# A running sum in one PSUM bank for the seven-product form, and a second group in four gate-and-up pairs of a decoder trunk

## The chip, the cores and the metric

The kernel runs on one core of a Trainium2 chip. The metric is the time of one execution on the device in microseconds (us), as the median of several runs. The profiled execution is a run of its own, with its own time. The engines are called as in the profile: PE (matrix products), PEld (loading of PE's stationary operand), DVE (vector), ACT (scalar), POOL (GpSimd) and SP (which here issues loads).

## The reference

The reference is a trunk of two decoder layers over 256 positions with 2048 channels, batch 1, all in float32. Of each layer only the products matter here:

```
h = rmsnorm(x);  proj = h @ w_in               # conv pair, q, k, v, two branch gates
m = sigmoid(g_A) * y_A + sigmoid(g_B) * y_B;   x += m @ w_out
gate, up = split(rmsnorm(x) @ w_gate_up)       # 2048 -> 2 x 5632
x += (silu(gate) * up) @ w_down                # 5632 -> 2048
x += sigmoid(rmsnorm(x) @ w_ple_gate) * (p[i] @ w_ple_proj)
```

y_A comes from a convolution branch, y_B from attention with eight heads. A last rmsnorm follows the second layer.

## The kernel before, in words

**Chunks and splits.** A weight matrix is cut into chunks of 512 output columns. The positions are two blocks of 128. The sum over the input rows is cut into groups of 512 rows (four tiles of 128). A half of a group, 256 rows by 512 columns, is one load of 512 KB into a raw tile (`fetch`, L133, issued by SP); there are eight raw tiles. Every float32 operand is split into a high part and a low part: `split` (L138) lets ACT copy raw to the high part wh (L141) and DVE subtract it to get the low part wl (L142). There are five wh and five wl tiles. A product of two split operands is three matmuls (L184, L185, L186): high times high, high times low and low times high. Activations are split in the same way and lie in pair tiles. A plain group of two chunks is four loads, four splits and 48 matmuls of 512 columns.

**The seven-product form.** `fast_chunks` (L238) takes two chunks w1 and w2 at once, and for some of the groups (the list `fast`) it uses seven products in place of eight. For one such group the blocks of the activations are B11, B12, B21, B22 (row halves of the group by position blocks) and those of the weights a11, a12 (from w1) and a21, a22 (from w2). The activation side has four sums, made once by `Fast.make` (L362): M1 = B11 - B12, T2 = M1 + B22, T3 = B22 - B12 and N4X = B21 - T2. On the weight side the tile sm starts as a21 and receives a11 by an accumulating load that POOL issues (L276). The seven products are, in the code's order:

- p1 = B11 with a11
- c21, N4X with a22
- c11, B21 with a12
- q7, T3 with sm, which is a21 + a11
- q6, T2 with sm after `add(sm, sm, a22)` (DVE, L287, recorded at the helper's line 271)
- q5, M1 with a11 after `sub(a11, sm, a11)` (L289, recorded at line 272)
- c12, B22 with a12 after `add(a12, a12, sm)` (L291, recorded at line 271)

Each is one split and six matmuls, 42 matmuls in all. c11, c12 and c21 are added in PSUM to the plain groups' sums. p1, q5, q6 and q7 have a bank of their own each (tiles ms; there are four). After the last group ACT copies p1 out (L293), and DVE makes from it p1 - q6, p1 - q6 + q7 and both of these plus q5 (L294 to L297), which are added to the plain sums or subtracted from them (L300, L304).

**The order of the work.** `go` is one plain step: it loads a half, splits it and multiplies it with both position blocks (12 matmuls). One or two such steps stand between the products of a group. After the groups come the rest of w1's plain steps, then the first result is used (`first`, L301), then w2's plain steps. Instructions are planned ahead of the run: each engine has a fixed order, close to that of the code, but an instruction whose operands are late by the planner's costs is overtaken by one that is ready. Tiles are handed out in that plan too, so a load waits in SP's queue until its raw tile is free.

**Where it is used.** There are 48 calls in the two layers: gates of the two branches, `w_out`, gate and up, down, and the last gate of a layer. The feed-forward part is done in three parts of 3, 4 and 4 chunks of 512 hidden columns (`FFN_PARTS`); in each part the gate-and-up pairs of its chunks come first, then the down projection. A gate-and-up pair uses two groups (L922), but the first pair of the second and third part uses one, and the first of the first part is plain. In all 80 groups run in the seven-product form.

Of the kernel before, what the change touches and what calls it, by code (L numbers as in the profile page):

```python
# [12 lines left out]
AF = mybir.ActivationFunctionType  # L13
ALU = mybir.AluOpType
# [31 lines left out]
def trunk(ctx, tc, xT, xR, pT, wI, wF, wC, wA, wOut, wGU, wD, wPG, wPP, vec, bF, gF, out):  # L46
    nc = tc.nc
# [11 lines left out]
    act, dve, pe = nc.scalar, nc.vector, nc.tensor  # L59
    uid = iter(range(1 << 30))  # L60

    def pair(dtype=F32):
        return pairs.tile([P, 2, 512], dtype, tag="pair", name=f"pair{next(uid)}")
# [69 lines left out]
    def fetch(src):  # L133
        raw = raws.tile([P, 2, 512], F32, tag="raw", name=f"raw{next(uid)}")
        nc.sync.dma_start(raw.rearrange("p k n -> p (k n)"), src)
        return raw
# [34 lines left out]


    class Sum:
        def __init__(self, n, bank):
            self.n, self.left, self.bank = n, n, bank

        @property
        def t(self):
# [2 lines left out]
        def add(self, xh, xl, wh, wl):  # L181
            start = self.left == self.n
            self.left -= 1
            pe.matmul(self.t, lhsT=xh, rhs=wh, start=start, stop=False)  # L184
            pe.matmul(self.t, lhsT=xh, rhs=wl, start=False, stop=False)  # L185
            pe.matmul(self.t, lhsT=xl, rhs=wh, start=False, stop=self.left == 0)  # L186

    def once(make):

        made = []  # L190

        def get():
            if not made:
                made.append(make())
            return made[0]

        return get

    def sums_of_blocks(n1, n2=None):
        t = once(bank_mm)  # L200
        return t, Sum(n1, lambda: t()[:, 0, :]), Sum(n1 if n2 is None else n2, lambda: t()[:, 1, :])
# [36 lines left out]
    def fast_chunks(fast, w1, w2, xs, ks, first, by_block=None):  # L238

        nf, nk = 2 * len(fast), 4 * len(ks)
        p1, q5, q6, q7 = (Sum(nf, once(bank_ms)) for _ in range(4))
        c1, c11, c12 = sums_of_blocks(nf + nk)
        c2, c21, c22 = sums_of_blocks(nf + nk, nk)
        if by_block is not None:
            c22 = Sum(nk, once(bank_ms))
        left = deque()
        for w, sums in ((w1, (c11, c12)), (w2, (c21, c22))):
            for g, k0 in enumerate(ks):  # L250
                for half in range(2):
                    left.append((w[len(fast) + g][:, half * 1024 : (half + 1) * 1024], sums, k0 + 2 * half))
        state = dict(quiet=True)

        def go(n=1):
            for _ in range(n):
                src, sums, k0 = left.popleft()
                parts = split(fetch(src))
                await_x(xs, (k0, k0 + 1))
                plain(sums, xs, k0, parts)  # L260
                if not state["quiet"]:
                    fill(CONV // 2 + len(left) % 2)
                    run()

        def product(to, operand, raw):
            h, l = split(raw)
            xh, xl = operand
            for kk in range(2):
                to.add(xh(kk), xl(kk), h[:, kk, :], l[:, kk, :])

        add = lambda o, a, b: dve.tensor_tensor(o, a, b, op=ALU.add)  # L271
        sub = lambda o, a, b: dve.tensor_tensor(o, a, b, op=ALU.subtract)  # L272
        u1, u2 = pair(), pair()
        for g, f in enumerate(fast):
            a11, sm = fetch(w1[g][:, :1024]), fetch(w2[g][:, :1024])
            nc.gpsimd.dma_start(sm.rearrange("p k n -> p (k n)"), w1[g][:, :1024], accum_op=ALU.add)  # L276
            a22, a12 = fetch(w2[g][:, 1024:]), fetch(w1[g][:, 1024:])
            product(p1, f(B11), a11)
            product(c21, f(N4X), a22)
            go()  # L280
            product(c11, f(B21), a12)
            if len(left) > 2 * len(ks):
                go()
            if nk == 8 and len(fast) == 1:
                run()
            product(q7, f(T3), sm)
            add(sm, sm, a22)  # L287
            product(q6, f(T2), sm)
            sub(a11, sm, a11)  # L289
            product(q5, f(M1), a11)  # L290
            add(a12, a12, sm)  # L291
            product(c12, f(B22), a12)
        act.activation(u1[:, 0, :], p1.t, AF.Copy)  # L293
        sub(u1[:, 1, :], u1[:, 0, :], q6.t)  # L294
        add(u2[:, 0, :], u1[:, 1, :], q7.t)
        add(u1[:, 1, :], u1[:, 1, :], q5.t)
        add(u2[:, 1, :], u2[:, 0, :], q5.t)  # L297
        state["quiet"] = False
        go(len(left) - 2 * len(ks))
        add(u1, u1, c1())  # L300
        first(u1)  # L301
        if by_block is None:
            go(len(left))
            sub(u2, c2(), u2)  # L304
            return u2
        go(len(left) - 4)
        held = [(split(fetch(src)), k0) for src, _, k0 in left]
        for b, c in enumerate((c21, c22)):
            for parts, k0 in held:
                plain([c, c], xs, k0, parts, [b])  # L310
            sub(u2[:, b, :], c.t, u2[:, b, :])
            by_block(b, u2)
# [25 lines left out]

        return (lambda b: o[:, b * P : (b + 1) * P]), (lambda b: o[:, S + b * P : S + (b + 1) * P])

    B11, B12, B21, B22, M1, T2, T3, N4X = range(8)

    class Fast:

# [17 lines left out]
        def make(self):  # L362
            f = lambda n: self.f[n // 4][:, n % 4]
            sub = lambda o, a, b, op: dve.tensor_tensor(f(o), f(a), f(b), op=op)  # L364
            sub(M1, B11, B12, ALU.subtract)
            sub(T2, M1, B22, ALU.add)
            sub(T3, B22, B12, ALU.subtract)
            sub(N4X, B21, T2, ALU.subtract)
            self.h, self.l = [], []
            for t in self.f:  # L370
                h, l = (pair(F32R).rearrange("p a b -> p (a b)") for _ in range(2))
                t = t.rearrange("p n k s -> p (n k s)")
                act.activation(h, t, AF.Copy)  # L373
                dve.tensor_tensor(l, t, h.bitcast(F32), op=ALU.subtract)  # L374
                self.h.append(h.rearrange("p (n k s) -> p n k s", n=4, k=2))
                self.l.append(l.rearrange("p (n k s) -> p n k s", n=4, k=2))
            self.f = None
# [167 lines left out]
    for i in range(L):  # L545
# [356 lines left out]
        c0 = 0  # L902
        for part, nch in enumerate(FFN_PARTS):
            hid = {}
            fast_hid = [Fast() for _ in range(nch - 2)]
            for c in range(c0, c0 + nch):
                w1, w2 = wGU[i, 2 * c], wGU[i, 2 * c + 1]
                o = pair() if c == 0 else None

                def gate(g):  # L910
                    nonlocal o
                    if o is None:
                        o = g
                    for b in range(2):
                        act.activation(o[:, b, :], g[:, b, :], AF.Silu, scale=norm.r(b))

                if c == 0:
                    gate(chunk(by_four(w1), norm.xs))
                    up = chunk(by_four(w2), norm.xs)
                else:  # L920
                    nf = 1 if c == c0 else 2
                    up = fast_chunks(norm.fast[:nf], w1, w2, norm.xs, range(4 * nf, KD, 4), gate)  # L922
                for b in range(2):
                    dve.scalar_tensor_tensor(
                        o[:, b, :], up[:, b, :], norm.r(b), o[:, b, :], op0=ALU.mult, op1=ALU.mult
                    )
                turns.append(
                    lambda c=c, o=o, hid=hid, fast=fast_hid[c - c0] if c - c0 < len(fast_hid) else None:
                    operand(hid, 4 * c, lambda b: o[:, b, :], fast)
                )  # L930
            for n in range(0, N4, 2):
                await_x(hid, (4 * c0,))
                on = after if part == len(FFN_PARTS) - 1 else None
                nf = 1 if n == 0 else len(fast_hid)
                onto_x(on, n + 1)(
                    fast_chunks(
                        fast_hid[:nf], wD[i, n][c0 : c0 + nch], wD[i, n + 1][c0 : c0 + nch], hid,
                        range(4 * (c0 + nf), 4 * (c0 + nch), 4), onto_x(on, n),
                    )
                )  # L940
            c0 += nch
            if part == len(FFN_PARTS) - 2:
                pin = tmp().rearrange("p (k s) -> p k s", k=2)
                nc.sync.dma_start(pin, pT[i])
                po = pair(F32R)
                halves(po, pin)
                ps = {k: by_blocks(po[:, k, :]) for k in range(2)}
# [119 lines left out]
```

## Time and profile before

| what | value |
|---|---|
| median of 3 runs | 2793.24 us (2793.18 to 2793.36) |
| profiled execution, its own time | 2793.7 us |
| its span, first to last instruction | 2791.8 us |
| PE, DVE, ACT busy | 2773.9, 2507.1, 1660.0 us |
| matmuls of 512 columns in L184 to L186 | 11712 |
| splits by ACT and DVE (L141, L142) | 1254 |
| DMA | 585.24 MB, mean 210 GB/s |

A row of a group reads: line, engine, operation, tile written <- tiles read, shape and count; then the busy time in us, the mean of one in ns, and the idle time of that engine just before these instructions, with what ended it. A row of waits reads: who waited <- for whom: us in total, times, longest. A row of the timeline has the start and the duration in us. A row of a stage has, after its bounds and its length, the busy time of each engine in it.

### The profile page before, as it was taken

What the parts mean: (1) busy time and instruction counts of PE and PEld (TensorE: products, weight loads), DVE (VectorE), ACT (ScalarE), POOL (GpSimd) and SP (SyncE); (2) the same over time, 40 slices, a digit from 0 to 9 for tenths busy, and PEclk for the clock granted to TensorE, in tenths of its full rate; (3) what the DMA queues carried; (4) which work ended last, traced back from release to release, by engine and by line L of the source; (5) the groups of instructions that cost most, each with busy time, mean ns of one, the idle gap of its engine ahead of it and who ended that gap; (6) DMA issues with size and microseconds to landing.
All of it is one profiled execution on the core that took longest, in us unless ns stands there. A gap on an engine that the chain in (4) does not pass through costs nothing.

```text
span 2791.8 us, 34941 instructions
## 1 busy us (share of the span) xinstructions
PE 2773.9 (99%) x12568; PEld 2293.5 (82%) x12568; DVE 2507.1 (90%) x3003; ACT 1660.0 (59%) x2002; POOL 79.4 (3%) x121
## 2 busy tenths in 40 slices
PE   9999999999999999999999999999999999999998
PEld 7888888888888888888888888888888888888886
DVE  7999889888989988999979988988799899889998
ACT  7445766565556655656754466655665565556565
POOL 0000000000000000000000000000000000000000
PEclk9999999999999999999999999999999999999999
DMA  7555557666676766776655555575666677677674
GB/s 299 188 182 185 199 186 227 198 217 201 217 226 220 227 218 220 224 221 203 215 186 190 185 181 199 189 233 184 228 205 215 216 232 231 203 229 218 217 239 131
DMA packets 161597, 585.24 MB, mean 210 GB/s; under 512 B 18192, under 2 KB 18448, under 8 KB 161168
## 3 DMA queue, kind: packets, MB, share of 16 engines
q1 hardware_dynamic: 149040, 539.50, 56.5%
q0 software_dynamic: 11520, 41.95, 8.3%
q8 instruction: 98, 1.61, 0.2%
q10 hardware_dynamic: 864, 1.57, 0.2%
q14 instruction: 75, 0.61, 0.1%
HBM read 580.85 MB, written 2.10 MB: 209 GB/s over the span
## 4 chain that ended last, share of the span: by engine, by line
PE 93%; DVE 3%; issue 3%; ACT 1%; POOL 0%; POOLq 0%; ACTq 0%; DVEq 0%
PE mm L186 25%; PE mm L185 25%; PE mm L184 25%; PE ms L184 5%; PE ms L185 5%; PE ms L186 5%; PE ms L334 2%; DVE wl L142 1%; DVE raw L271 0%; PE ms L726 0%; ACT wh L141 0%; PE ms L755 0%; DVE pair L374 0%; PE ms L745 0%; DVE pair L271 0%
## 5 line engine op out<-in xcount | busy, mean ns | idle before, releaser
L141 ACT ACTIVATE wh<-raw 128x1024 fp32r<-128x1024 f32 x1254 | 1300.5, 1058 | 1022.7 <-PE mm L186 576.7
L142 DVE TENSOR_TENSOR wl<-raw,wh 128x1024 fp32r<-128x1024 f32 x1254 | 1501.0, 1219 | 212.4 <-ACT wh L141 204.9
L184 PE MATMUL mm<-wh,pair 128*128 128x512 f32 x3224 | 1261.9, 392 | 1.1 <-ACT pair L324 0.7
L185 PE MATMUL mm<-wl,pair 128*128 128x512 f32 x3224 | 1256.6, 390 | 0.9 <-DVE wl L142 0.8
L186 PE MATMUL mm<-wh,pair 128*128 128x512 f32 x3224 | 1256.8, 390 | 0.5 <-DVE pair L325 0.5
L186 PEld LDWEIGHTS mm<-wh,pair 128*128 128x128 f32 x3224 | 605.2, 188 | 128.4 <-DVE pair L325 1.4
L185 PEld LDWEIGHTS mm<-wl,pair 128*128 128x128 f32 x3224 | 605.6, 188 | 126.3 <-DVE wl L142 3.2
L184 PEld LDWEIGHTS mm<-wh,pair 128*128 128x128 f32 x3224 | 605.4, 188 | 126.0 <-ACT pair L324 1.7
L184 PE MATMUL ms<-wh,pair 128*128 128x512 f32 x680 | 265.7, 391 | 0.1
L186 PE MATMUL ms<-wh,pair 128*128 128x512 f32 x680 | 264.7, 389 | 0.0
L185 PE MATMUL ms<-wl,pair 128*128 128x512 f32 x680 | 264.6, 389 | 0.0
L569 DVE SCALAR_TENSOR_TENSOR pair<-pair,vecs,pair 128x256 f32<-128x256 f32 x480 | 201.1, 474 | 0.0
L271 DVE TENSOR_TENSOR raw<-raw,raw 128x1024 f32<-128x1024 f32 x160 | 195.4, 1222 | 2.6
L184 PEld LDWEIGHTS ms<-wh,pair 128*128 128x128 f32 x680 | 127.7, 188 | 28.0 <-ACT pair L998 0.9
L186 PEld LDWEIGHTS ms<-wh,pair 128*128 128x128 f32 x680 | 127.6, 188 | 26.7
L185 PEld LDWEIGHTS ms<-wl,pair 128*128 128x128 f32 x680 | 127.7, 188 | 26.0
L272 DVE TENSOR_TENSOR raw<-raw,raw 128x1024 f32<-128x1024 f32 x80 | 98.0, 1225 | 2.6
L271 DVE TENSOR_TENSOR pair<-pair,ms 128x512 f32<-128x512 f32 x144 | 93.9, 680 | 0.0
L272 DVE TENSOR_TENSOR pair<-mm,pair 128x1024 f32<-128x1024 f32 (+1 forms) x48 | 58.1, 1210 | 11.5 <-PE mm L186 11.4
L271 DVE TENSOR_TENSOR pair<-pair,mm 128x1024 f32<-128x1024 f32 x48 | 58.3, 1215 | 5.5 <-PE mm L186 5.5
L374 DVE TENSOR_TENSOR pair<-pair,pair 128x1024 fp32r<-128x1024 f32 x52 | 62.8, 1217 | 0.0
L373 ACT ACTIVATE pair<-pair 128x1024 fp32r<-128x1024 f32 x52 | 54.3, 1055 | 2.7 <-DVE pair L364 1.6
(168 smaller groups left out, 1065.0 us busy)
## 6 DMA issues: line engine op xcount, KB each, us to landing
raw<-in_wGU_dram SPq DMA_DIRECT2D x352, 512.0 KB, 4.8
raw<-in_wI_dram SPq DMA_DIRECT2D x287, 512.0 KB, 4.0
raw<-in_wD_dram SPq DMA_DIRECT2D x176, 512.0 KB, 4.8
raw<-in_wOut_dram SPq DMA_DIRECT2D x64, 512.0 KB, 4.6
raw<-in_wPG_dram SPq DMA_DIRECT2D x64, 512.0 KB, 4.9
raw<-in_wGU_dram POOLq DMA_DIRECT2D x36, 512.0 KB, 7.9
raw<-in_wA_dram SPq DMA_DIRECT2D x32, 512.0 KB, 4.7
raw<-in_wC_dram SPq DMA_DIRECT2D x32, 512.0 KB, 4.9
```

The lines of the kernel that those rows point to most:

```text
L141: act.activation(h, raw, AF.Copy)
L142: dve.tensor_tensor(l, raw, h.bitcast(F32), op=ALU.subtract)
L184: pe.matmul(self.t, lhsT=xh, rhs=wh, start=start, stop=False)
L185: pe.matmul(self.t, lhsT=xh, rhs=wl, start=False, stop=False)
L186: pe.matmul(self.t, lhsT=xl, rhs=wh, start=False, stop=self.left == 0)
L271: add = lambda o, a, b: dve.tensor_tensor(o, a, b, op=ALU.add)
L272: sub = lambda o, a, b: dve.tensor_tensor(o, a, b, op=ALU.subtract)
L334: pe.transpose(pt[:, kk * S + b * P : kk * S + (b + 1) * P], src(b)[:, c : c + P], ident)
L373: act.activation(h, t, AF.Copy)
L374: dve.tensor_tensor(l, t, h.bitcast(F32), op=ALU.subtract)
L569: dve.scalar_tensor_tensor(cv[c], u[c][:, j : j + S], w, cv[c], op0=ALU.mult, op1=ALU.add,)
```

## The change

Two things are changed.

1. The results p1, q6 and q7 get one bank, `chain`, in which they become a running sum. p1 of all groups is multiplied first; ACT copies the bank (p1). Then, group by group, the products with NT2, which is -T2, are added to it; ACT copies it again (p1 - q6). At the end the products with T3 are added, and ACT copies it a third time (p1 - q6 + q7). DVE only adds q5 to two of these. For that `Sum` gets a third argument, the number of places at which the sum may be read, and `Fast.make` makes NT2 in place of T2. The tile sm stays a21 + a11 up to the end, where T3 is multiplied with it; the weight sum for NT2 is written over a22. The accumulating load of the second group is issued within the first group's turn. The tiles u1 and u2 are taken later.
2. The first gate-and-up pair of the second and third part uses two groups, as the others do (`nf = 2`). Over two layers that is four pairs.

```diff
     class Sum:
-        def __init__(self, n, bank):
-            self.n, self.left, self.bank = n, n, bank
+        def __init__(self, n, bank, rests=1):
+
+            self.n, self.left, self.bank, self.rest = n, n, bank, n // rests
...
-            pe.matmul(self.t, lhsT=xl, rhs=wh, start=False, stop=self.left == 0)
+            kw = dict(skip_group_check=self.rest < self.n)
...
+            pe.matmul(self.t, lhsT=xl, rhs=wh, start=False, stop=self.left % self.rest == 0, **kw)
...
-        p1, q5, q6, q7 = (Sum(nf, once(bank_ms)) for _ in range(4))
+        chain, q5 = Sum(3 * nf, once(bank_ms), 3), Sum(nf, once(bank_ms))
...
-        u1, u2 = pair(), pair()
+        def third(g):
+            sm = fetch(w2[g][:, :1024])
+            nc.gpsimd.dma_start(sm.rearrange("p k n -> p (k n)"), w1[g][:, :1024], accum_op=ALU.add)
+            return sm
+
+        s3 = [third(0)]
+        a11s = []
         for g, f in enumerate(fast):
-            a11, sm = fetch(w1[g][:, :1024]), fetch(w2[g][:, :1024])
-            nc.gpsimd.dma_start(sm.rearrange("p k n -> p (k n)"), w1[g][:, :1024], accum_op=ALU.add)
+            a11s.append(fetch(w1[g][:, :1024]))
+            product(chain, f(B11), a11s[g])
+        u1 = pair()
+        act.activation(u1[:, 0, :], chain.t, AF.Copy)
+        for g, f in enumerate(fast):
+            a11, sm = a11s[g], s3[g]
             a22, a12 = fetch(w2[g][:, 1024:]), fetch(w1[g][:, 1024:])
-            product(p1, f(B11), a11)
             product(c21, f(N4X), a22)
             go()
             product(c11, f(B21), a12)
...
-            product(q7, f(T3), sm)
-            add(sm, sm, a22)
-            product(q6, f(T2), sm)
-            sub(a11, sm, a11)
+            if g < len(fast) - 1:
+                s3.append(third(g + 1))
+            add(a22, sm, a22)
+            product(chain, f(NT2), a22)
+            if g == len(fast) - 1:
+                act.activation(u1[:, 1, :], chain.t, AF.Copy)
+            sub(a11, a22, a11)
             product(q5, f(M1), a11)
-            add(a12, a12, sm)
+            add(a12, a12, a22)
             product(c12, f(B22), a12)
-        act.activation(u1[:, 0, :], p1.t, AF.Copy)
-        sub(u1[:, 1, :], u1[:, 0, :], q6.t)
-        add(u2[:, 0, :], u1[:, 1, :], q7.t)
+        for sm, f in zip(s3, fast):
+            product(chain, f(T3), sm)
         add(u1[:, 1, :], u1[:, 1, :], q5.t)
+        u2 = pair()
+        act.activation(u2[:, 0, :], chain.t, AF.Copy)
         add(u2[:, 1, :], u2[:, 0, :], q5.t)
...
-            sub(T2, M1, B22, ALU.add)
             sub(T3, B22, B12, ALU.subtract)
-            sub(N4X, B21, T2, ALU.subtract)
+            dve.scalar_tensor_tensor(f(NT2), f(M1), -1.0, f(B22), op0=ALU.mult, op1=ALU.subtract)
+            sub(N4X, B21, NT2, ALU.add)
...
-                    nf = 1 if c == c0 else 2
+                    nf = 2
```

More of the change, by code (lines that the diff above doesn't have):

```diff
@@ L183, in add @@
             self.left -= 1
-            pe.matmul(self.t, lhsT=xh, rhs=wh, start=start, stop=False)
-            pe.matmul(self.t, lhsT=xh, rhs=wl, start=False, stop=False)
-            pe.matmul(self.t, lhsT=xl, rhs=wh, start=False, stop=self.left == 0)
+            kw = dict(skip_group_check=self.rest < self.n)
+            pe.matmul(self.t, lhsT=xh, rhs=wh, start=start, stop=False, **kw)
+            pe.matmul(self.t, lhsT=xh, rhs=wl, start=False, stop=False, **kw)
+            pe.matmul(self.t, lhsT=xl, rhs=wh, start=False, stop=self.left % self.rest == 0, **kw)
     def once(make):
@@ L339, in by_blocks @@
         return (lambda b: o[:, b * P : (b + 1) * P]), (lambda b: o[:, S + b * P : S + (b + 1) * P])
-    B11, B12, B21, B22, M1, T2, T3, N4X = range(8)
+    B11, B12, B21, B22, M1, NT2, T3, N4X = range(8)
     class Fast:
```

## Prediction

> **What bounds the kernel now.** I read the page's first two parts, then its costliest groups, then the waits, then busy times by stage.
>
> ```profile
> span 2791.8 us, 34941 instructions
> PE 2773.9 (99%) x12568; PEld 2293.5 (82%) x12568; DVE 2507.1 (90%) x3003; ACT 1660.0 (59%) x2002; POOL 79.4 (3%) x121
> PEclk9999999999999999999999999999999999999999
> L142 DVE TENSOR_TENSOR wl<-raw,wh 128x1024 fp32r<-128x1024 f32 x1254 | 1501.0, 1219 | 212.4 <-ACT wh L141 204.9
> L141 ACT ACTIVATE wh<-raw 128x1024 fp32r<-128x1024 f32 x1254 | 1300.5, 1058 | 1022.7 <-PE mm L186 576.7
> ```
>
> PE is busy in every slice at full clock. DVE is second with 90%, an average that hides what matters below. A busy PE isn't proof that it is at its pace, so I take the pace from the timeline. These two rows, from a stretch of back-to-back products, stand 8 rounds of three matmuls (L184, L185, L186) apart:
>
> ```profile
> 774.07 0.39 PE L184 MATMUL mm<-wh,pair 128*128 128x512 f32 x1
> 779.51 0.39 PE L184 MATMUL mm<-wh,pair 128*128 128x512 f32 x1
> ```
>
> 24 matmuls take 779.51 - 774.07 = 5.44 us, so 0.2267 us each. The 0.39 us is the length of one, overlapped with the next. All 11712 such matmuls (3 x 3224 into mm banks, 3 x 680 into ms banks) take 2655 us of the 2791.8 at this pace; most of the rest is transposes, attention and the two ends. What PE waits for in between is little:
>
> ```profile
> ACT wh L141 <- PE mm L186: 576.7, 421, 2.7
> ACT wh L141 <- DVE raw L271: 316.1, 142, 4.9
> PEld mm L185 <- DVE wl L142: 3.2, 7, 0.9
> PEld ms L334 <- DVE xt L881: 2.2, 6, 0.8
> ACT wh L141 <- DMA raw<-in_wGU_dram: 2.2, 1, 2.2
> ```
>
> The producers wait for PE, hardly ever PE for them, and a split waited for a gate-and-up load once. So PE's matmul count is the time, as long as DVE keeps up. The busy times of one first gate-and-up pair (layer 0, part 2) and the two pairs behind it, cut at PE's own borders:
>
> ```profile
> core 0: us, PE busy (x) PEld busy (x) DVE busy (x) ACT busy (x) POOL busy (x), PEclk, DMA share, GB/s
> 790.40:832.56 42.16, 42.16 (x188) 34.92 (x187) 31.93 (x29) 21.45 (x22) 1.70 (x2) 1.00 0.72 224
> 832.56:874.28 41.72, 41.72 (x190) 34.62 (x188) 41.24 (x42) 27.41 (x29) 1.70 (x2) 1.00 0.64 204
> 874.28:916.00 41.72, 41.72 (x189) 34.61 (x188) 41.43 (x42) 27.13 (x29) 1.25 (x2) 1.00 0.72 226
> ```
>
> The first pair, with one group, uses 31.93 of 42.16 us of DVE. The pairs with two groups use 41.24 and 41.43 of 41.72: there DVE has no room at all.
>
> **The second group in four pairs.** A group of 512 rows costs 8 products of 6 matmuls the plain way and 7 in the seven-product form. Two layers with two parts each give 4 pairs, so 4 x 6 = 24 matmuls go, which is just the 5.44 us of the rows above; one pair falls from 186 to 180 matmuls, 42.16 to 40.8 us. [...]
>
> What the group adds: 7 splits in place of 4 and three adds on raw tiles.
>
> ```profile
> L271 DVE TENSOR_TENSOR raw<-raw,raw 128x1024 f32<-128x1024 f32 x160 | 195.4, 1222 | 2.6
> L271 DVE TENSOR_TENSOR pair<-pair,ms 128x512 f32<-128x512 f32 x144 | 93.9, 680 | 0.0
> L272 DVE TENSOR_TENSOR pair<-pair,ms 128x512 f32<-128x512 f32 x48 | 32.6, 680 | 0.0
> L293 ACT ACTIVATE pair<-ms 128x512 f32<-128x512 f32 x48 | 27.7, 578 | 0.0
> L364 DVE TENSOR_TENSOR pair<-pair,pair 128x256 f32<-128x256 f32 x52 | 21.7, 418 | 1.9 <-ACT pair L358 1.8
> L569 DVE SCALAR_TENSOR_TENSOR pair<-pair,vecs,pair 128x256 f32<-128x256 f32 x480 | 201.1, 474 | 0.0
> ```
>
> On DVE that is 3 x 1.22 for splits and 3 x 1.22 for adds, 7.3 us a pair; on ACT 3 x 1.06 = 3.2 us; one more accumulating load of 512 KB on POOL's queue, which is 3% busy. DVE in the first pair then needs 31.93 + 7.3 = 39.2 of 40.8 us before the other part of the change helps. The cover is the 10.2 us in which DVE is idle there now. If it were not usable, because it lies in the plain stretch that is halved, the pair would run at DVE's pace and give back up to its 1.36 us.
>
> **The running sum, in all 48 calls.** Of the four DVE instructions that combine p1, q5, q6 and q7, the subtract of q6 and the add of q7 go: 2 x 0.68 = 1.36 us of DVE a call, 65 us in all. Two more ACT copies of 0.578 come: 1.16 us a call, 55 us in all, on an engine that is 59% busy. PE's products are the same. Beside the first pair's 7.3 us the saving leaves DVE 37.9 of 40.8 us; for the steady pairs 41.24 - 1.36 = 39.9 of 41.72. So DVE stays behind PE as the bound. NT2 by a scalar-tensor-tensor costs at most 474 - 418 = 56 ns more in each of the operands made, under 2 us of DVE in the program and hidden. What the freed time is worth on PE: at most the 3.2 us for splits, whose seven waits lie partly at the start and in attention; I take 0.3 us, one such wait:
>
> ```profile
> 737.51 1.24 DVE wl L142
> 738.79 0.50 PE mm L185
> ```
>
> It is in the chain of waits, and this L185 starts when DVE ends; the pace would have been 0.23.
>
> **Waits that the sum adds.** The bank must be read between its products. The first copy has c21, a plain step, c11 and a second step behind p1 before NT2 writes (36 matmuls, 8.2 us, in a call with two groups). The second copy has only q5 and c12 before T3: 12 matmuls, 2.72 us. Queued on ACT around it are splits; one or two ahead of it make 0.58 + 1.06 or 0.58 + 2.12 = 2.70 us. So its cost is 0 up to two splits ahead, and about 1.06 us a call with three. I take 0, since ACT must itself wait for PE before a sixth split (five tiles of each kind).
>
> **What moves on the queues.** In a two-group call SP's order becomes sm, a11, the second a11, then a22, a12, two plain loads, and sm of the second group. This moves the second a11 ahead of four loads; all hold raw tiles, of which there are eight. sm now stays until T3 at the end, and a22 takes the place of sm as the tile that is added to. Loads already wait for tiles:
>
> ```profile
> SPq L135 <- DVE wl L142: 1666.7, 786, 9.4
> raw<-in_wGU_dram SPq DMA_DIRECT2D x352, 512.0 KB, 4.8
> raw<-in_wGU_dram POOLq DMA_DIRECT2D x36, 512.0 KB, 7.9
> ```
>
> The tightest load is the second group's first plain one. Today it starts when the first add frees a22; afterwards a22 is free only after the third:
>
> ```profile
> 879.89 1.23 DVE L271 TENSOR_TENSOR raw<-raw,raw 128x1024 f32<-128x1024 f32 x1
> 881.14 0.33 SPq L135 DMA_DIRECT2D raw<-in_wGU_dram  x1
> 883.45 1.22 DVE L271 TENSOR_TENSOR raw<-raw,raw 128x1024 f32<-128x1024 f32 x1
> 891.96 0.19 PEld L185 LDWEIGHTS mm<-wl,pair 128*128 128x128 f32 x1
> ```
>
> The split of T3 and its product, and p1 of the second group, leave this stretch. The third add then ends about 1.2 us sooner than 884.67, at 883.5, and PE wants the tile 2 x 1.36 us sooner than 891.96, at 889.24. With 4.8 us to land and 1.06 + 1.22 for the split it is ready at 890.6: 1.4 us late. If c11, whose load isn't late, is put ahead of it (1.36 us of PE), it is on time within 0.05 us. The price is thus 0 to 1.4 us in each of 36 two-group calls (32 now and 4 new). I take 0, nearest to the row of today, in which no split waits for such a load, because the order is planned before the run and a planner that sees the tile come late puts the ready product first. The second sm is still the eighth tile and has c21, two plain steps and c11 more before its use, over 8 us.
>
> Sum: -5.44 - 0.3 = -5.7 us. The profiled execution took 2793.7 us (span 2791.8 and 1.9 around it), so 2788.0; the median of the runs is 0.46 us below the profiled one, so **2787.5 us**.
>
> **Rivals.**
> 1. Late loads, slower. Mechanism and place as above: eight raw tiles, the plain load after the third add. Break-even is 5.7 / 36 = 0.16 us a call; at 0.4 us, that is at 5.2 us to land without the better order, 14.4 - 5.7 = +8.7 us, 2802. For it: the 1666.7 us that loads wait for tiles. Against it: one wait for a gate-and-up load in the whole trace.
> 2. The bank, slower. T3 waits for the second copy, with three splits ahead of it: 48 x 1.06 = 51 us, 2838. Against it: in the row of L293 today's copies had 0.0 us of idle time before them. [...]
> 3. The cover is gone: the first pairs run at DVE's pace and all 5.44 us are given back, 2793. For it: two-group pairs fill DVE to 99% today. Against it: 2.9 us of room after both parts.
> 4. More than the matmuls: the freed DVE time also ends most waits for splits and residuals, 2 us, 2785.8.
>
> That the change doesn't do what it says can't be for the count: 24 matmuls fewer is fixed by the code.
>
> **How the numbers follow.** A measurement of this kernel can tell about 0.2%, 5.59 us, from no change: the border is 2787.65, almost on my forecast. Forecast (gain between 4.4 and 6.7): 0.55, of which 0.35 falls over the border. Rival 4: 0.08. A gain partly or wholly eaten (rival 3, or small waits): 0.19. Rivals 1 and 2 beyond 0.2%: 0.12 and 0.06. Faster 0.35 + 0.08 = 0.43; same 0.20 + 0.19 = 0.39; slower 0.18. The range goes from rival 4's 2785.8 to 2796.0, where late loads cost 0.23 us in 36 calls; beyond it lie most of the slower cases. The forecast's own range is 2786.5 to 2788.8.
>
> **What would show it.** Right: 11688 large matmuls at 0.227 us; the four first pairs at 40.8 us; DVE near 2507 - 65 + 29 = 2471 us and ACT near 1660 + 55 + 13 = 1728; waits of PE as short as now. Wrong: waits of splits for loads in every call (rival 1); PE weight loads into ms banks waiting for an ACT copy (rival 2); DVE over 99% in the first pairs with PE waiting for wl (rival 3).

## The result, and the profile after

| kernel | median | runs | ratio to before |
|---|---|---|---|
| before | 2792.91 us | 2792.5 to 2793.36 (9) | |
| after | 2799.91 us | 2795.47 to 2802.23 (9) | 1.0023 (95%: 1.0013 to 1.0033) |

The change makes the kernel 7.0 us slower, 0.23%, where the forecast was 5.7 us faster and the range ended at 2796.0. The profiled execution of after took 2801.55 us, 7.85 more than that of before. Its page begins:

```profile
span 2799.8 us, 35090 instructions
...
PE 2772.3 (99%) x12544; PEld 2291.1 (82%) x12544; DVE 2475.0 (88%) x2931; ACT 1716.6 (61%) x2110; POOL 82.2 (3%) x125
```

The 24 matmuls are gone (12568 to 12544), and DVE has lost 32 us of work. Yet the span is 8.0 us longer. At 0.2267 us each, 24 matmuls are 5.44 us, so PE should be busy for 2773.9 - 5.4 = 2768.5 us; it is busy for 2772.3, 3.8 us more. Its idle time went from 2791.8 - 2773.9 = 17.9 us to 27.5, 9.6 us more. These 13.4 us are what has to be found. The stages come first, since the group could have used up DVE's room in the first pairs; the columns are the bounds, the length, then each engine's busy time, PE's clock, the DMA share and GB/s:

```profile
791.71:832.51 40.80, 40.80 (x181) 33.78 (x180) 37.19 (x34) 25.14 (x27) 1.30 (x2) 1.00 0.72 231
832.51:874.24 41.73, 41.73 (x190) 34.61 (x188) 39.17 (x40) 28.12 (x31) 1.55 (x3) 1.00 0.74 227
```

The first pair takes 40.80 us where it took 42.16, and DVE has room in both. The waits of after, in us in total, times, and the longest, PE's, DVE's, ACT's and then the load queue's:

```profile
PE mm L186 <- DVE pair L274: 7.4, 4, 2.1
PE mm L187 <- DVE wl L142: 3.5, 4, 1.6
...
DVE raw L273 <- DMA raw<-in_wD_dram: 8.1, 6, 2.4
...
ACT wh L141 <- DMA raw<-in_wGU_dram: 46.0, 30, 2.5
ACT wh L141 <- DMA raw<-in_wI_dram: 19.3, 8, 4.8
...
SPq L135 <- DVE wl L142: 1889.3, 882, 12.3
SPq L135 <- DVE raw L273: 157.8, 65, 5.9
```

The same view of before has two rows to set against them:

```profile
PE mm L185 <- DVE wl L142: 0.8, 3, 0.5
...
SPq L135 <- DVE raw L271: 461.9, 154, 6.9
```

Four things are new. PE waits four times, 7.4 us in all, for DVE to read a finished bank (L274, the subtraction `sub(u2, c2(), u2)` at the end of a call). PE waits 2.7 us more for low parts of splits. DVE's adds on raw tiles wait for loads of the down projection. And splits on ACT wait for gate-and-up loads 30 times, where it was once. In SP's queue the waits for a raw add became waits for a split (wl): fewer raw tiles are now freed by an add, and more by a split.

**Where PE waits.** The four waits are at the passage from the last gate-and-up pair of a part to its first down call. One of them, in layer 0, second part, in the timeline of before (start, duration, engine, line):

```profile
945.83 0.84 POOL L276 DMA_DIRECT2D raw<-in_wD_dram  x1 [29.37 <-DMA raw<-in_wD_dram]
957.97 1.23 DVE L272 TENSOR_TENSOR pair<-mm,pair 128x1024 f32<-128x1024 f32 x1 [0.35 <-PE mm L186]
962.82 1.22 DVE L271 TENSOR_TENSOR raw<-raw,raw 128x1024 f32<-128x1024 f32 x1
```

The accumulating load is issued at 945.83. DVE reads the bank as soon as PE has finished it, at 957.97, and gets to the first raw add of the down call at 962.82. In after:

```profile
940.37 0.33 SPq L135 DMA_DIRECT2D raw<-in_wD_dram  x1
945.73 0.86 POOL L277 DMA_DIRECT2D raw<-in_wD_dram  x1 [29.00 <-DVE wl L142]
955.04 1.23 DVE L273 TENSOR_TENSOR raw<-raw,raw 128x1024 f32<-128x1024 f32 x1 [0.96 <-DMA raw<-in_wD_dram]
956.19 1.22 DVE L142 TENSOR_TENSOR wl<-raw,wh 128x1024 fp32r<-128x1024 f32 x1
957.32 1.22 DVE L274 TENSOR_TENSOR raw<-raw,raw 128x1024 f32<-128x1024 f32 x1
958.46 1.22 DVE L142 TENSOR_TENSOR wl<-raw,wh 128x1024 fp32r<-128x1024 f32 x1
959.71 1.23 DVE L273 TENSOR_TENSOR raw<-raw,raw 128x1024 f32<-128x1024 f32 x1
960.85 1.22 DVE L274 TENSOR_TENSOR pair<-mm,pair 128x1024 f32<-128x1024 f32 x1
962.21 0.47 PE L186 MATMUL mm<-wh,pair 128*128 128x512 f32 x1 [1.64 <-DVE pair L274]
```

The load is issued at the same time and lands at 954.95. But the add of the down call now stands 8 us earlier in DVE's fixed order, ahead of the bank. DVE stands for the load, then does the call's three adds and the splits between them, and reads the bank at 960.85. PE, which wants that bank, stands for 1.64 us. The six passages, from the traces, in us (landing of the first accumulating load of the down call, start of its first add, start of the read-out):

| passage | before: landing, add, read-out | after | nine_raws (below) |
|---|---|---|---|
| layer 0, part 1 | 723.78, 731.50, 726.65 | 723.56, 723.65, 729.46 | 718.42, 720.22, 726.47 |
| layer 0, part 2 | 955.94, 962.82, 957.97 | 954.95, 955.04, 960.85 | 947.39, 949.68, 955.93 |
| layer 0, part 3 | 1207.88, 1214.12, 1209.27 | 1206.32, 1206.41, 1212.22 | 1197.15, 1199.55, 1205.80 |
| layer 1, part 1 | 2109.91, 2118.50, 2113.64 | 2115.02, 2115.12, 2120.92 | 2103.66, 2104.49, 2110.74 |
| layer 1, part 2 | 2341.81, 2349.87, 2345.02 | 2346.60, 2346.69, 2352.50 | 2331.76, 2333.95, 2340.20 |
| layer 1, part 3 | 2593.03, 2601.16, 2596.31 | 2598.88, 2598.98, 2604.78 | 2581.48, 2583.82, 2590.07 |

In before the read-out always comes first, and the add 6 to 9 us after the landing. In after the add comes first, and starts 0.09 to 0.10 us after the landing in all six: it is always the load that lets DVE go on, and the read-out follows 5.8 us behind. The loads themselves land when they did, in layer 1 some 5 us later, where DVE's work before the passages is already 3.9 to 5.6 us late. The code says why the add could move: in before `add(sm, sm, a22)` writes over sm and so had to stay behind both instructions of q7's split; in after `add(a22, sm, a22)` leaves sm as it is, and besides the loads only a22's split must be done.

**What is behind 2.1 us.** Another of the four, in layer 1, as PE's timeline and the stage behind it have it:

```profile
2122.29 0.58 PE L186 MATMUL mm<-wh,pair 128*128 128x512 f32 x1 [2.14 <-DVE pair L274]
2122.66 0.63 PE L187 MATMUL mm<-wl,pair 128*128 128x512 f32 x1
2123.09 0.63 PE L188 MATMUL mm<-wh,pair 128*128 128x512 f32 x1
```

```profile
2122.50:2125.90 3.40, 3.40 (x9) 2.65 (x9) 3.40 (x5) 0.00 (x0) 0.00 (x0) 0.50 0.42 154
```

After the stop the granted clock is 0.50 for 3413 ns; matmuls stand 0.43 us apart (2123.09 - 2122.66) where they stood 0.227. That is 3.41 x (1 - 0.227 / 0.43) = 1.6 us more, behind a wait of 2.14. From the first product to the last matmul it happens twice in the profile (2122.5 and 2607.2). The last 8.2 us of before's profile and the last 8.3 us of after's are at half clock too, but PE has no work left in them.

So 13.3 of the 13.4 us have a name: 7.4 for the bank, 2.7 for low parts (1.6 of them in one wait at the last gate of layer 0, see "Still open"), 3.2 at half clock.

The loss can also be followed by marks: DVE's read-outs of finished sums, 48 in the program, each compared with its time in before. The read-out above is 960.85 - 957.97 = 2.88 us late; the one of the pair before was 0.15 late, so the step is +2.73. The steps at the six passages, and at the last gate of layer 0, in us:

| place | after | sum_only | order_held | no_accum | nine_raws | group_only |
|---|---|---|---|---|---|---|
| layer 0, part 1 | +2.77 | +3.15 | +0.51 | +0.70 | +0.70 | -0.07 |
| layer 0, part 2 | +2.73 | +1.42 | +0.83 | +1.16 | +1.42 | -0.03 |
| layer 0, part 3 | +1.84 | +1.40 | +1.52 | +1.65 | +1.40 | -0.01 |
| layer 1, part 1 | +3.38 | +2.26 | +0.35 | +0.87 | +0.70 | -0.07 |
| layer 1, part 2 | +1.93 | +1.95 | +0.72 | +1.55 | +1.38 | -0.04 |
| layer 1, part 3 | +3.18 | +2.04 | +1.19 | +1.36 | +1.40 | -0.02 |
| sum of the six | 15.8 | 12.2 | 5.1 | 7.3 | 7.0 | -0.2 |
| last gate, layer 0 | +3.34 | +3.71 | +3.47 | +2.75 | +1.90 | +0.01 |

A step of a mark isn't yet a loss: where PE doesn't wait, it is only DVE's order. In after the six steps and the gate come to 19.2 us, the four first pairs to -5.8, and the calls in between give 5.3 back. That leaves the last mark 8.1 us late; the spans differ by 8.0.

### The profile page after: what moved, and what is told of

It reads as the page before. It is cut to its first block, busy times and chain, and to the rows that moved or that the text cites. A ratio compares the mean times of both kernels' runs of the same rounds, so it can differ in the third digit from the quotient of the medians.

```text
span 2799.8 us, 35090 instructions
## 1 busy us (share of the span) xinstructions
PE 2772.3 (99%) x12544; PEld 2291.1 (82%) x12544; DVE 2475.0 (88%) x2931; ACT 1716.6 (61%) x2110; POOL 82.2 (3%) x125
## 4 chain that ended last, share of the span: by engine, by line
PE 87%; DVE 5%; DMA 4%; issue 2%; ACT 1%; SPq 0%; POOLq 0%; ACTq 0%; DVEq 0%; POOL 0%
PE mm L186 23%; PE mm L188 23%; PE mm L187 23%; PE ms L186 5%; PE ms L187 5%; PE ms L188 5%; DVE wl L142 3%; DMA raw<-in_wD_dram 2%; PE ms L349 2%; ACT wh L141 1%; DMA raw<-in_wGU_dram 1%; DVE raw L274 1%; DMA raw<-in_wI_dram 0%; PE ms L741 0%; DVE pair L274 0%
## 5 line engine op out<-in xcount | busy, mean ns | idle before, releaser
L186 PE MATMUL mm<-wh,pair 128*128 128x512 f32 x3184 | 1247.7, 392 | 7.9 <-DVE pair L274 7.4
L187 PE MATMUL mm<-wl,pair 128*128 128x512 f32 x3184 | 1243.0, 390 | 3.5 <-DVE wl L142 3.5
L188 PE MATMUL mm<-wh,pair 128*128 128x512 f32 x3184 | 1241.9, 390 | 0.6 <-DVE pair L340 0.5
L186 PEld LDWEIGHTS mm<-wh,pair 128*128 128x128 f32 x3184 | 598.6, 188 | 132.8 <-ACT wh L141 10.0
L188 PEld LDWEIGHTS mm<-wh,pair 128*128 128x128 f32 x3184 | 598.5, 188 | 127.4 <-DVE pair L340 1.2
L187 PEld LDWEIGHTS mm<-wl,pair 128*128 128x128 f32 x3184 | 598.6, 188 | 127.0 <-DVE wl L142 5.3
L186 PE MATMUL ms<-wh,pair 128*128 128x512 f32 x712 | 277.7, 390 | 0.0
L187 PE MATMUL ms<-wl,pair 128*128 128x512 f32 x712 | 277.1, 389 | 0.0
L188 PE MATMUL ms<-wh,pair 128*128 128x512 f32 x712 | 277.1, 389 | 0.0
L273 DVE TENSOR_TENSOR raw<-raw,raw 128x1024 f32<-128x1024 f32 x168 | 205.0, 1220 | 10.9 <-DMA raw<-in_wD_dram 8.1
L186 PEld LDWEIGHTS ms<-wh,pair 128*128 128x128 f32 x712 | 133.6, 188 | 28.4 <-ACT pair L1013 0.8
L188 PEld LDWEIGHTS ms<-wh,pair 128*128 128x128 f32 x712 | 133.6, 188 | 27.8
L274 DVE TENSOR_TENSOR raw<-raw,raw 128x1024 f32<-128x1024 f32 x84 | 102.5, 1220 | 1.0
L273 DVE TENSOR_TENSOR pair<-pair,ms 128x512 f32<-128x512 f32 x96 | 65.4, 681 | 10.4 <-PE ms L188 10.2
L274 DVE TENSOR_TENSOR pair<-mm,pair 128x1024 f32<-128x1024 f32 (+1 forms) x48 | 57.9, 1206 | 1.9 <-PE mm L188 1.8
```

The costliest lines, as they stand in the source:

```text
L186: pe.matmul(self.t, lhsT=xh, rhs=wh, start=start, stop=False, **kw)
L187: pe.matmul(self.t, lhsT=xh, rhs=wl, start=False, stop=False, **kw)
```

## The experiments

Two theories had to be told apart. By one (theory A in the texts on record), the loss is in DVE's planned order: the next call's adds stand ahead of the read-out. By the other, the late loads of the prediction's first rival (theory B), it is in the tiles: sm is held until T3 and a22 through the third add, so that eight raw tiles are too few. Each kernel ran in five rounds beside before, whose medians in the three batches were 2792.72, 2792.44 and 2792.58 us.

| kernel | median, us | runs | ratio (95%) |
|---|---|---|---|
| group_only | 2787.59 | 2786.96 to 2788.23 (11) | 0.9982 (0.9973 to 0.9990) |
| sum_only | 2799.11 | 2797.30 to 2804.25 (8) | 1.0027 (1.0016 to 1.0037) |
| order_held | 2791.41 | 2790.38 to 2793.42 (11) | 0.9996 (0.9987 to 1.0004) |
| nine_raws | 2785.25 | 2784.71 to 2786.04 (9) | 0.9974 (0.9964 to 0.9983) |
| group_nine | 2787.70 | 2787.27 to 2788.12 (11) | 0.9982 (0.9973 to 0.9991) |
| nine_kept | 2798.53 | 2797.58 to 2799.65 (11) | 1.0021 (1.0012 to 1.0030) |
| no_accum | 2787.85 | 2786.42 to 2788.70 (11) | 0.9983 (0.9974 to 0.9992) |
| group_seven | 2811.45 | 2810.53 to 2812.04 (5) | 1.0066 (1.0054 to 1.0079) |
| sum_nine | 2790.53 | 2790.06 to 2791.18 (11) | 0.9993 (0.9983 to 1.0002) |
| nine_held | 2785.01 | 2784.90 to 2785.65 (7) | 0.9973 (0.9962 to 0.9984) |
| ten_raws | 2785.54 | 2784.83 to 2786.26 (8) | 0.9974 (0.9964 to 0.9985) |

**group_only**: before with the second group alone.

```diff
-                    nf = 1 if c == c0 else 2
+                    nf = 2
```

> The four banks of before, with the second group in the four first pairs alone. Theory A (the planned order: in the changed kernel adds on raw tiles of the next call stand on DVE ahead of the subtraction that empties the last bank of the call before; here none does): the 24 matmuls are gained in full, 2792.9 - 5.4 = 2787.5 us. Theory B (eight raw tiles are too few, loads come late): about the same, 2787 to 2790. Theory D (DVE cannot carry a second group in the first pairs without the running sum): little or no gain, 2791 to 2794, with DVE over 99% in those pairs.

It gains 5.1 us. Its first pair, by stages, and ACT's waits for gate-and-up loads:

```profile
790.25:831.05 40.80, 40.80 (x181) 33.78 (x180) 38.47 (x35) 24.74 (x25) 1.52 (x3) 1.00 0.76 230
```

```profile
ACT wh L141 <- DMA raw<-in_wGU_dram: 1.2, 3, 0.7
```

DVE has 38.47 us of work in 40.80, without any help from the sum, and no load is late. The group needs no cover from the other part.

**sum_only**: after without the second group.

```diff
-                    nf = 2
+                    nf = 1 if c == c0 else 2
```

> The running sum alone, one group in the first pairs as before. Changed against before by 7.0 us with 5.4 us of matmuls saved, so the sum would have to cost 12.4 us. Theory A, and B and C (PE waits for the ACT copies of the bank): 2792.9 + 12.4 = 2805 us, 2801 to 2808, under A with PE's waits at the passage from the gate-and-up pairs to the down projection, under C spread over all 48 calls. Theory D: 2793, the loss lying in the first pairs.

It loses 6.4 us, nearly what the whole change loses, but only half of the 12.4 forecast: beside the group the sum costs 12.3 us (2799.91 - 2787.59), by itself 6.4. In its profile PE waits 3.4 us for the bank where after has 7.4, and the granted clock is 0.999 over the span, as in before, where after's is 0.997. PE's and ACT's waits of it:

```profile
PE mm L186 <- DVE pair L274: 3.4, 3, 1.9
```

```profile
ACT wh L141 <- DMA raw<-in_wGU_dram: 35.9, 25, 3.0
```

Both signs of after are here. The running sum is the loser; which of its consequences, the next two kernels ask.

**order_held**: after, with the first add of each group held behind the read-out of the call before.

```diff
-            add(a22, sm, a22)
+            if last_sub:
+                with tc.issue_after(last_sub[-1].ins):
+                    add(a22, sm, a22)
+            else:
+                add(a22, sm, a22)
...
-            sub(u2, c2(), u2)
+            last_sub.append(sub(u2, c2(), u2))
```

> The changed kernel, with one order held on DVE: the first add on a raw tile of a call stays behind the subtraction that empties the last bank of the call before. No wait is added, no tile changed. Theory A: the long waits of PE at the end of the gate-and-up pairs (8.3 us for that subtraction, and two drops of the clock of 1.7 us each behind them) go, and 2788 us, 2786 to 2791, is reached. Theories B and C: nothing of theirs is touched, so 2797 to 2802.

8.5 us come back (2799.91 to 2791.41); theory A's range ended at 2791. PE's wait for the read-out is gone from its waits (7.4 us in after, not the 8.3 of the expectation); what is left is late loads:

```profile
PE mm L187 <- DVE wl L142: 5.5, 7, 1.6
```

```profile
ACT wh L141 <- DMA raw<-in_wGU_dram: 56.8, 36, 4.1
```

So the order carries most of the loss at eight tiles, but not all: order_held is still 3.8 us behind group_only.

**nine_raws**: after with a ninth raw tile, paid for with one pair tile of the same size.

```diff
-PAIRS = 28
+PAIRS = 27
...
-RAWS = 8
+RAWS = 9
```

> The changed kernel with nine raw tiles in place of eight (and 27 pair tiles in place of 28, to make room). Theory A: the adds stand as far ahead as before in the plan, so the waits at the passages stay, 2796 to 2802 us. Theory B: loads have a tile each when they are wanted, 2787 to 2790 us. Theory C: 2797 to 2802.

14.7 us come back, 1.8 more than theory B's range, and the kernel beats before by 7.5 us. The passage from above, in the timeline of this kernel:

```profile
933.66 0.33 SPq L135 DMA_DIRECT2D raw<-in_wD_dram  x1
937.26 0.86 POOL L277 DMA_DIRECT2D raw<-in_wD_dram  x1 [26.03 <-DVE wl L142]
949.68 1.22 DVE L273 TENSOR_TENSOR raw<-raw,raw 128x1024 f32<-128x1024 f32 x1
955.93 1.22 DVE L274 TENSOR_TENSOR pair<-mm,pair 128x1024 f32<-128x1024 f32 x1
```

The order on DVE is still the planned one, add first and read-out behind it. But the load is issued 6.7 us earlier (933.66, was 940.37), 3.6 of which are the lead that this kernel has over after by then. The add waits for nothing, and PE's waits hold no L274. PE's and ACT's waits of it:

```profile
PE mm L187 <- DVE wl L142: 2.8, 3, 1.6
```

```profile
ACT wh L141 <- DMA raw<-in_wGU_dram: 3.7, 3, 1.7
```

It is so at all six passages: the add starts 0.8 to 2.4 us after its load has landed. The 46.0 us for which splits waited for gate-and-up loads are 3.7. PE's longest wait is 1.6 us, and the granted clock is 0.998 over the span (0.997 in after).

**group_nine**: is a ninth tile good for anything in the four-bank form? group_only with the two lines of nine_raws.

```diff
-PAIRS = 28
+PAIRS = 27
...
-RAWS = 8
+RAWS = 9
...
-                    nf = 1 if c == c0 else 2
+                    nf = 2
```

> The control for the nine tiles: the four banks of before, a second group in the four first pairs, nine raw tiles and 27 pair tiles. Theory B (the running sum keeps raw tiles longer, so loads start late; nine tiles give that back): nothing comes late with four banks and eight tiles, so no gain, 2787 to 2788.2 us. Theory E (a ninth tile helps any version by the same): as much as it helped the changed kernel, 14.7 us, or at least a few us, below 2785.

It isn't: 2787.70 against 2787.59. So nine_raws doesn't gain by tiles in general; the sum needs one more.

**sum_nine**: the sum alone with nine tiles (sum_only with the two lines).

```diff
-PAIRS = 28
+PAIRS = 27
...
-RAWS = 8
+RAWS = 9
...
-                    nf = 2
+                    nf = 1 if c == c0 else 2
```

> The running sum alone (one group in the first pairs) with nine raw tiles. If late loads are the whole price of the sum (theory B), the sum is then worth what nine tiles left of it in the changed kernel, 2785.25 - 2787.6 = -2.3 us: 2790.2, 2789 to 2791.5. If the sum has a cost of its own beside the loads (copies of the bank, theory C): 2792.7 or more.

It gains 2.1 us, where sum_only lost 6.4. With nine tiles the parts add up: the group -4.7 (group_nine against before) or -5.3 (nine_raws against sum_nine), the sum -2.1 (sum_nine against before) or -2.5 (nine_raws against group_nine), both together -7.5.

**ten_raws**: one more of the same kind.

```diff
-PAIRS = 28
+PAIRS = 26
...
-RAWS = 8
+RAWS = 10
```

> The changed kernel with ten raw tiles and 26 pair tiles. Theory B: splits waited 7.4 us for weight loads in all with nine, so little is left, 2784 to 2785.5. If tiles are still short: 2780 to 2783. If 26 pair tiles are too few, slower than 2786.

2785.54 us, no further gain: nine are enough.

**nine_held**: does the order still cost anything when no load is late? order_held with the two lines of nine_raws.

```diff
-PAIRS = 28
+PAIRS = 27
...
-RAWS = 8
+RAWS = 9
```

> The changed kernel with nine raw tiles and the first add of a call held behind the subtraction that empties the last bank before it, and nothing else held. Theory B, by which order matters only where loads come late: 2784.5 to 2786, as nine tiles alone. Theory A: the 1.4 us at each of six passages go, 2778 to 2782. If the adds standing ahead are of use by themselves: 2787 to 2790.

2785.01 against 2785.25 us: nothing that could be measured. So the order at the passages is harmless by itself; at eight tiles it is what turns late loads into a stop of PE.

**no_accum**: after without the accumulating load; sm holds a21 alone, so the sums lack a11 in T3 and behind it.

```diff
-            nc.gpsimd.dma_start(sm.rearrange("p k n -> p (k n)"), w1[g][:, :1024], accum_op=ALU.add)
```

> The changed kernel without the accumulating load: the tile sm holds the second chunk's block alone, so the weight sums lack the first chunk's block, and one load in three of a group's tail is gone; the order on DVE is the same as in the changed kernel, adds ahead included. If the accumulating load that comes late is the whole of it: 2785 to 2788 us. Theory B, where plain loads come late too because tiles are short: the drops of the clock and the longest waits go, the waits of ACT for plain loads stay, 2789 to 2796. Theory A (the order alone, whether loads are late or not): 2797 to 2801.

12.1 us come back, which is in the range given for the accumulating load as the whole of it, though plain loads still come late, as theory B said. What is left to nine_raws is 2.6 us, and the waits of ACT point to plain loads:

```profile
ACT wh L141 <- DMA raw<-in_wGU_dram: 40.6, 29, 3.2
```

So plain loads are about as often late as in after (46.0 us, 30 times), and by this run that costs little; the dear one is the accumulating load. The kernel also moves 44 MB less, all of them this load's, so its 12.1 us are an upper bound for its lateness.

**group_seven**: the same shortage made in the four-bank form, group_only with seven raw tiles.

```diff
-RAWS = 8
+RAWS = 7
...
-                    nf = 1 if c == c0 else 2
+                    nf = 2
```

> The four banks of before with a second group in the four first pairs, and seven raw tiles in place of eight. Theory B: taking a tile away does to this form what the running sum does by keeping one longer, 2787.6 + 4 to 12, so 2791 to 2800 us, with waits of ACT for loads as in the changed kernel (some 80 us in all). Theory A: the order on DVE has no add ahead, so at most 2789.

One tile less costs 23.9 us (2811.45 - 2787.59), twice the upper end of the 4 to 12 forecast and more than the lack of one costs the sum alone (2799.11 - 2790.53 = 8.6). Its waits of PE and of ACT look as after's do:

```profile
PE mm L184 <- DVE pair L272: 8.2, 7, 1.4
```

```profile
ACT wh L141 <- DMA raw<-in_wGU_dram: 46.4, 38, 2.2
ACT wh L141 <- DMA raw<-in_wD_dram: 22.5, 14, 3.8
ACT wh L141 <- DMA raw<-in_wI_dram: 17.3, 16, 1.6
```

A bank wait (here L272) can come without the running sum, from the tiles alone: around the read-out at 921.72 DVE has the same order as in group_only, with no add ahead of it. The four-bank form sat right on the edge: eight were enough for it and seven were not.

**nine_kept**: nine tiles, with the first add kept at its place in the code, a blunter way to hold the order.

```diff
-            add(a22, sm, a22)
+            tc.keep_in_program_order(add(a22, sm, a22))
```

> The changed kernel with nine raw tiles, and the first add on a raw tile of each group held on DVE behind the instruction traced before it, so that no add of the next call stands ahead of the read-out of the last bank. With loads in time, what order is worth by itself: the passages from gate-and-up to down still lose 1.4 us each and the last gate of layer 0 1.9 us with nine tiles; if the adds standing ahead do that, these 6 to 10 us go in part and 2780 to 2784 us is reached; if the order only matters where loads come late (theory B), 2784.5 to 2786.5, as with nine tiles alone.

It loses all of the gain, by an accident of this edit. DVE's waits and the timeline at the first down call of layer 0:

```profile
DVE pair L337 <- ACT pair L336: 15.0, 4, 6.9
```

```profile
736.57 1.29 DVE L337 TENSOR_TENSOR pair<-ms,pair 128x512 fp32r<-128x512 f32 x2 [6.90 <-ACT pair L336]
737.77 1.22 DVE L273 TENSOR_TENSOR raw<-raw,raw 128x1024 f32<-128x1024 f32 x1
```

In that call the code makes the rest of the down projection's operands (`run()`) ahead of the add, and the pin keeps the add behind them while they wait for ACT and PE. The read-out marks step by 6.86 and 6.48 us at this call in the two layers, 13.3 us in all, and its time is 13.3 us above that of nine_raws. The run misses both forecasts and says nothing on the order at the passages; nine_held does.

## Why the prediction was wrong

**PE's pace and the 24 matmuls: right.** 40.80 us in the first pair as worked out (40.8), and 5.1 us in group_only for 5.44.

**DVE's room: right, with margin.** Forecast 37.9 of 40.8 us in the first pair and 39.9 in the steady ones; measured 37.19 and 39.17. Over the program DVE was forecast at 2471 us and is busy for 2475.0; ACT at 1728, with 1716.6. Rival 3, the lost cover, falls with group_only.

**The bank read between its products: right, at nothing.** ACT's copies wait for PE in small pieces, and no row of PE's waits names one of the copies; rival 2 falls. ACT's waits:

```profile
ACT pair L286 <- PE ms L188: 11.0, 38, 0.3
```

**The 0.3 us for splits: wrong in after, too small in principle.** PE waited 2.7 us more for low parts. With enough tiles the sum gained 2.1 us, and nine_raws at 2785.25 is near rival 4's 2785.8, but not by rival 4's way: PE's waits for low parts did not shrink (2.8 us in nine_raws, 0.8 in before). The profiled spans differ by 2.2 us (2783.3 in nine_raws, 2785.5 in group_nine); where in them the gain lies was not shown.

**What moves on the queues: the step that failed.** The prediction saw that a22 and sm would be held longer, priced the second group's first plain load at 0 to 1.4 us, and took 0, "nearest to the row of today", "because the order is planned before the run and a planner that sees the tile come late puts the ready product first". In place of 0, the want of a ninth tile cost 14.7 us (2799.91 against nine_raws' 2785.25). Three things are wrong in the step.

1. The row of today showed that hardly a split waited; it did not show how much was to spare. It was less than one tile, which group_seven prices at 23.9 us.
2. The plan did not help, it hurt: it put the add that waits for the late load ahead of the read-out that PE wants. Why its costs put the landing so early wasn't looked into. That the order is what turns the wait into PE's is shown by order_held (8.5 us).
3. The place was wrong. Inside the two-group calls, where I looked, plain loads do get late, and that costs little (no_accum still has them). The price is paid at the passages to the down projection, and there by a load that isn't late at all by the clock of before: its first add comes about 8 us sooner (in layer 0 at 723.65, was 731.50). I followed who frees each tile, and never asked how much earlier the new code lets each tile be read.

**Rival 1** thus had half of the mechanism: too few tiles for the loads, which a ninth heals; not the half that the order adds. Its 2802 us lies near the result, but it reached it with 0.4 us in each of 36 calls; the trace has 15.8 us of steps at six passages and 3.3 at one gate. Its own figures slip, too: with 5.2 us to land the tile is ready at 883.5 + 5.2 + 2.28 (the split's 1.06 + 1.22) = 890.98, which is 0.4 us late only with c11 put ahead (889.24 + 1.36 = 890.60); without that better order it is 1.7 us late. That the total came near the result is luck. The chance of 0.12 came from the same row read as room to spare. The range ended where its cost was 0.23 us a call, and so was too short.

**Still open.** The step at the last gate of layer 0 (+3.34 in after, +1.90 with nine tiles, only +0.26 in layer 1) was not tried by itself. The timeline of after shows an early add there too. It stands behind the read-out (1347.46), but ahead of a split that PE wants:

```profile
1349.85 1.23 DVE L273 TENSOR_TENSOR raw<-raw,raw 128x1024 f32<-128x1024 f32 x1
1350.99 1.22 DVE L980 TENSOR_TENSOR pair<-pair,pair 128x1024 f32<-128x1024 f32 x1
1352.13 1.22 DVE L142 TENSOR_TENSOR wl<-raw,wh 128x1024 fp32r<-128x1024 f32 x1
1353.40 0.50 PE L187 MATMUL mm<-wl,pair 128*128 128x512 f32 x1 [1.60 <-DVE wl L142]
```

This stop of 1.60 us is in nine_raws and nine_held as well (order_held's edit does not reach it), and not in before. In nine_kept, which keeps that add back, it is 0.76 us and the step is +0.96. By that comparison the early add costs about 0.8 us there; the rest stays open. And that after's spread of 6.8 us, where before has 0.9, comes from stops behind which half clock follows in some executions and not in others was not shown: the granted clock is 0.997 in the three slowest executions and 0.998 in the other six, but only the profiled one has a trace.

## What to carry to other kernels

When an edit takes a dependency away, ask which instruction may now be planned earlier, whether its load is there by then, and what stands behind it in its engine's fixed order: that wait is paid by all of them (here by the read-out, for which PE waited 7.4 us). "No wait today" is not a margin; taking one buffer away shows how much there is. And before giving up a change that saves work but holds buffers longer, try one buffer more: here it turned 7.0 us lost into 7.5 gained.

## What the runs showed of the hardware

Of PE's four waits for a finished bank in after, the two longest were followed by 3413 ns at a granted clock of 0.50: one of 2.14 us, with the fall 0.2 us behind its end (2122.29 and 2122.50), and one of 2.04 us, with the fall 1.0 us behind it (2606.15 and 2607.19). The other two, of 1.53 and 1.64 us, were not, nor was the longest in sum_only, of 1.9 us (granted clock 0.999 over the span). In nine_kept PE's longest wait at the first down call of layer 0 was 3.9 us, and 6.80 us there (739.30 to 746.10) were at 0.50, as were 6.80 us at this call in layer 1 (2128.50 to 2135.30). The stop of 2.14 us so cost nearly 4 here, with the 1.6 us at half clock.

A 512 KB load that accumulates took 9.22 us at the passage (945.73 to 954.95). The median of such loads of this tensor is 8.5 us in after (9.3 in before), that of plain loads 5.7 (4.8 in before). So a tile that is made by two loads, one behind the other, was there 14.6 us after its first request (940.37 to 954.95).
